# Gathered tokens of a product-key expert layer: joined to the output as rows, or turned and added in the closing stores

## The chip, the cores and the metric

The kernel runs on one core of a Trainium2 chip. The metric is the device time of one execution in microseconds (us), as the median of several runs. A profiled execution of the kernel before is read here as well; its own time stands beside its span below.

## What is computed

One decoder layer on 512 tokens of width 2048, all in float32. The part that matters here is its end: an expert feed-forward part (PEER) with 16384 experts, each one row of `expert_u` and one of `expert_v`, of which each token uses 8 x 16 = 128:

```python
x   = x + gate1 * (concat[y_c, y_a] @ W_out)              # called x1 in the kernel
h2  = RMSNorm(x) * (1 + scale2) + shift2
# idx, g: 128 experts and gates of each token, from product keys
a   = einsum('thkd,td->thk', expert_u[idx], h2)
ffn = einsum('thk,thkd->td', gelu(a) * g, expert_v[idx])
x   = x + gate2 * ffn
```

## The kernel before

Activations are kept transposed: a tile holds 128 of the 2048 features in its partitions and the tokens side by side. Every float32 product is made of three passes over a high and a low part (PASSES); `split` (L87) makes the two parts, the high one on ScalarE (L88), the low one by a subtraction on VectorE or GpSimd (L89).

**Stages.** Modulation and attention come first. Then the output projection (L529 to L561): four column groups dg of 512 features; each brings its part of x in, turns it (L535, L537, PSUM tiles `px` with two buffers), multiplies (L547), and forms x1 = x + gate1 * product on VectorE (L553), stored to `x1_dram` (L554) and squared for the norm (L559, L561). After the last group follow the sums of squares (L569), the root (L571, L572), its broadcast by eight small products into another `px` tile (L575), and h2 (L586 to L592). L586 overwrites x1 in place. Then come queries (L701) and selection of experts.

**Two ways for the expert part.** The 512 tokens are divided. The first TG = 160 are *gathered*: each fetches its own rows of the expert tables with indirect DMAs. The other TD = 352 are *dense*: all 16384 experts are multiplied with them, and a matrix W holds the gates.

The dense pass has 16 chunks of CH = 8 expert blocks. Of each block, `u_block` (L784) multiplies the turned rows of expert_u (loaded as `ur`, turned on VectorE L780, split) with h2 (L792), and `w_block` (L816) applies the gates and makes W. Then `v_group(ch, dg)` (L930) runs for the four column groups: four loads `vr` of expert_v (three buffers, L934), four splits `vs` (two buffers, L939), 24 products each (L945), summed in two PSUM tiles `pv` out of a pool of three (L924). The sums of the chunks are added up in `acc` (L959, L961).

Beside this, `steps` (L879) lists the gathers, and `gather_to` (L888) places them by the progress of the dense pass; each waits in GpSimd's queue for a product noted in `pace` (L847). A step fetches 128 half rows of 1024 values (512 KB) into one of four buffers `gt` (GBUF = 4, L843). The first group is tokens 0 to 127: 128 experts in two halves, first expert_u (dot products on VectorE, L853), then, after `gather_w`, expert_v (added up on VectorE into `gacc`, tokens in the partitions, L867 and L869). `gather_next` (L871) stores gacc to `a_dram` (L872) and loads what the second group needs. That group has the last nb = 32 gathered tokens, folded four times over the partitions: 32 experts for each quarter, so gacc then holds four partial sums of each token.

**The end.** In the last chunk, `begin(dg)` (L966) loads x1 of all tokens of a column group into `xs`, and adds acc times gate2 for the dense tokens (L972); after the group's products the last chunk's sums are added (L953). `add_gathered(dg)` (L975) reloads the first group's sums from a_dram (L978), turns them (L984), turns gacc (L988), copies both (L986, L989), adds the three other quarters (L991) and adds all to xs (L993). `store(dg)` (L996) turns xs back to rows (L1002, in a `pv` tile), copies (L1005 on VectorE, L1007 on ScalarE) and writes 512 columns of each 128 tokens out (L1008). ADD_AT and STORE_AT say after which dg this is done.

**What sets the order.** All loads and stores are issued by SP in one queue, the gathers by GpSimd. A planner (the tile framework) takes the program in the order in which it is written, estimates when each instruction can run, and fixes the order of every engine's queue; each engine then works through its queue in that order. Buffers of a pool are handed out in the order of the program. `add_manual_dep(..., ORDER)` tells the planner that one instruction comes after another.

## Time and profile before

| | |
|---|---|
| median of 3 runs | 3521.41 us (3520.7 to 3525.29) |
| the profiled execution | 3524.61 us, span 3522.6 us |
| mean granted TensorE clock | 0.967 |
| TensorE, VectorE, ScalarE, GpSimd busy | 92%, 81%, 35%, 40% |
| mean DMA rate over the span | 254 GB/s |
| output projection | about 795 to 967 us |
| first gather, first gather of the second group, last gather issued | 1455.0, 3072.3, 3458.0 us |

The span is the time from the first to the last instruction. Engines are PE (TensorE), DVE (VectorE), ACT (ScalarE), POOL (GpSimd) and SP, which only issues DMAs. A wait is put down to the instruction that released it last. [...]

### The profile page before, as it was taken

The page shows a single profiled execution, that of the slowest core. Times are in us where ns is not written, and L with a number is a line of the kernel's source. Part 1 is how long each engine was busy: PE and PEld are TensorE (multiplying, and loading weights), DVE is VectorE, ACT ScalarE, POOL GpSimd, SP SyncE. Part 2 cuts the span into 40 slices and gives each one's busy share as a digit, 9 for nine tenths or more (in the row PEclk, how much of TensorE's full clock was granted, in tenths as well). Part 3 has the DMA queues.
Part 4 walks back from the last instruction along what each step waited for, and adds up shares of the span by engine and source line. Part 5 has one row for each costly group of instructions (what it writes and reads, how often), then busy time and mean ns, then how long its engine had stood idle before and what let it go on. Part 6 is the DMA issues. An engine that isn't in the chain of part 4 may idle for free.

```text
span 3522.6 us, 49092 instructions
## 1 busy us (share of the span) xinstructions
PE 3223.4 (92%) x18006; PEld 2970.3 (84%) x18006; DVE 2847.1 (81%) x4261; ACT 1220.5 (35%) x1828; POOL 1417.5 (40%) x985
## 2 busy tenths in 40 slices
PE   5888999999998797999999999999999999999985
PEld 4766777677787686899998999889999999999975
DVE  6789766653269999789898888888999898988885
ACT  5232334343264357423232232223233232332221
POOL 2447332254447420134443444333434444444441
PEclk9999999999999899999999999999999999999987
DMA  8864755559722135899999999999999999999984
GB/s 288 286 229 143 254 190 178 183 177 290 252 88 68 61 122 202 264 298 323 305 315 295 310 310 299 300 287 300 306 314 313 298 307 306 326 310 319 299 302 163
DMA packets 425712, 896.34 MB, mean 254 GB/s; under 512 B 40402, under 2 KB 119167, under 8 KB 420735
## 3 DMA queue, kind: packets, MB, share of 16 engines
q1 hardware_dynamic: 333310, 557.62, 52.3%
q0 software_dynamic: 92160, 335.59, 29.3%
q8 instruction: 141, 2.31, 0.3%
q14 instruction: 101, 0.82, 0.1%
HBM read 843.47 MB, written 49.55 MB: 254 GB/s over the span
## 4 chain that ended last, share of the span: by engine, by line
DMA 42%; DVE 28%; PE 15%; issue 9%; POOL 3%; SPq 2%; ACT 1%; DVEq 0%; POOLq 0%; ACTq 0%
DMA ur<-in_expert_u_dram 14%; DMA vr<-in_expert_v_dram 9%; DMA gt<-in_expert_u_dram,idxu 6%; PE pm L457 4%; DMA ada_w<-in_w_ada_dram 4%; DMA gt<-in_expert_v_dram,idxu 4%; DVE gacc L869 3%; DVE utf L780 3%; DVE vs L89 2%; DVE gt L907 2%; DVE gt L853 2%; DVE ut L89 2%; DVE ada_acc L196 2%; PE pm L547 2%; DVE run L196 2%
## 5 line engine op out<-in xcount | busy, mean ns | idle before, releaser
L792 PE MATMUL pa<-hd,ut 128*128 128x352 f32 x6144 | 1077.3, 328 | 63.9 <-DVE ut L89 41.0
L945 PE MATMUL pv<-W,vs 128*128 128x352 f32 x6144 | 1071.4, 328 | 50.6 <-DVE vs L89 27.0
L792 PEld LDWEIGHTS pa<-hd,ut 128*128 128x128 f32 x6144 | 1015.2, 191 | 75.8 <-DVE ut L89 48.4
L945 PEld LDWEIGHTS pv<-W,vs 128*128 128x128 f32 x6144 | 1014.5, 191 | 61.2 <-DVE vs L89 32.7
L89 POOL TENSOR_TENSOR wsp<-wraw,wsp 128x1024 fp32r<-128x1024 f32 x160 | 391.5, 2449 | 562.1 <-ACT wsp L88 530.3
L844 POOL DMA_INDIRECT gt<-in_expert_u_dram,idxu x256 | 343.9, 1344 | 626.4 <-DVE gt L853 309.8
L88 ACT ACTIVATE vs<-vr 128x1024 fp32r<-128x1024 f32 x256 | 271.3, 1060 | 819.2 <-DMA vr<-in_expert_v_dram 365.8
L844 POOL DMA_INDIRECT gt<-in_expert_v_dram,idxu x256 | 340.0, 1328 | 477.9 <-DVE gacc L869 341.5
L853 DVE SCALAR_TENSOR_TENSOR gt<-gt,h2n 128x1024 f32<-128x1024 f32 x320 | 386.2, 1215 | 104.9 <-DMA gt<-in_expert_u_dram,idxu 84.8
L869 DVE SCALAR_TENSOR_TENSOR gacc<-gt,ga_a,gacc 128x1024 f32<-128x1024 f32 x316 | 400.4, 1275 | 73.9 <-DMA gt<-in_expert_v_dram,idxu 48.5
L89 DVE TENSOR_TENSOR vs<-vr,vs 128x1024 fp32r<-128x1024 f32 x256 | 309.8, 1210 | 46.9 <-ACT vs L88 46.7
L88 ACT ACTIVATE ut<-utf 128x1024 fp32r<-128x1024 f32 x232 | 244.0, 1056 | 282.3 <-DVE utf L780 169.6
L780 DVE STREAM_TRANSPOSE utf<-ur 128x1024 f32<-128x1024 f32 x232 | 286.9, 1237 | 18.2 <-DMA ur<-in_expert_u_dram 14.1
L88 ACT ACTIVATE wsp<-wraw 128x1024 fp32r<-128x1024 f32 x160 | 169.1, 1058 | 368.1 <-issue 94.7
L89 DVE TENSOR_TENSOR ut<-utf,ut 128x1024 fp32r<-128x1024 f32 x232 | 281.9, 1215 | 9.6 <-ACT ut L88 9.5
L457 PE MATMUL pm<-big,wsp 128*128 128x512 f32 x1152 | 287.6, 402 | 0.0
L457 PEld LDWEIGHTS pm<-big,wsp 128*128 128x128 f32 x1152 | 215.2, 192 | 42.6 <-issue 0.2
L196 DVE SCALAR_TENSOR_TENSOR ada_acc<-ada_w,scol,ada_acc 128x512 f32<-128x512 f32 x195 | 208.3, 1068 | 28.5 <-DMA ada_w<-in_w_ada_dram 25.1
L245 PE MATMUL pqk<-wsp,big 128*128 128x512 f32 x768 | 193.3, 411 | 21.3 <-DVE qk L291 12.9
L701 PE MATMUL pm<-big,wsp 128*128 128x512 f32 x768 | 188.2, 402 | 16.1 <-POOL wsp L89 14.5
L245 PEld LDWEIGHTS pqk<-wsp,big 128*128 128x128 f32 x768 | 150.6, 199 | 57.6 <-DVE qk L291 15.9
L701 PEld LDWEIGHTS pm<-big,wsp 128*128 128x128 f32 x768 | 146.2, 193 | 48.5 <-POOL wsp L89 17.0
(274 smaller groups left out, 3195.4 us busy)
## 6 DMA issues: line engine op xcount, KB each, us to landing
vr<-in_expert_v_dram SPq DMA_DIRECT2D x256, 512.0 KB, 10.0
ur<-in_expert_u_dram SPq DMA_DIRECT2D x928, 128.0 KB, 9.2
ada_w<-in_w_ada_dram SPq DMA_DIRECT2D x192, 512.0 KB, 4.6
wraw<-in_w_in_dram SPq DMA_DIRECT2D x96, 512.0 KB, 5.0
g_dram<-gtile SPq DMA_DIRECT2D x11, 2048.0 KB, 7.1
g<-g_dram SPq DMA_DIRECT2D x32, 704.0 KB, 13.6
wraw<-in_w_out_dram SPq DMA_DIRECT2D x32, 512.0 KB, 5.1
wraw<-in_w_peer_q_dram SPq DMA_DIRECT2D x32, 512.0 KB, 3.7
```

The costliest lines, as they stand in the source:

```text
L88: hi = nc.scalar.activation(dst[:, 0], src, AF.Copy)
L89: (eng or nc.vector).tensor_tensor(out=dst[:, 1], in0=src, in1=dst[:, 0].bitcast(F32), op=OP.subtract)
L196: nc.vector.scalar_tensor_tensor(new, wt[:, k], s, old, op0=OP.mult, op1=OP.add)
L245: nc.tensor.matmul(banks[i], hT[kk][:, a, i * P:(i + 1) * P], ws[:, b, k], start=(kk == last[0] and n == 0), stop=(kk == last[1] and n == 2))
L457: nc.tensor.matmul(banks[n2], ws[:, a, k, n2 * P:(n2 + 1) * P], hT[kk][:, b], start=(kk == 0 and n == 0), stop=(kk == KC - 1 and n == 2))
L701: nc.tensor.matmul(banks[j], ws[:, a, k, j * P:(j + 1) * P], h2T[kk][:, b], start=(kk == 0 and n == 0), stop=(kk == KC - 1 and n == 2))
L780: nc.vector.transpose(t, UR[0][:, :, q * 256:(q + 1) * 256].rearrange("p b (c r) -> p c b r", r=32))
L792: mm = nc.tensor.matmul(pa[:, :TD], ut[:, a, j], hd[k][:, b], start=(k == 0 and n == 0), stop=(k == KC - 1 and n == 2))
L844: d = nc.gpsimd.indirect_dma_start(out=t, out_offset=None, in_=src, in_offset=bass.IndirectOffsetOnAxis(ap=gidx[g][:, j:j + 1], axis=0), e ...
L853: nc.vector.scalar_tensor_tensor(t, t, 1.0, h2n[:, f * D // 2:(f + 1) * D // 2], op0=OP.mult, op1=OP.mult, accum_out=ga_a[:, f, j:j + 1])
L869: nc.vector.scalar_tensor_tensor(gacc[:, s], t, a, gacc[:, s], op0=OP.mult, op1=OP.add)
L945: mm = nc.tensor.matmul(pv[j // 2][:, j % 2, :TD], vs[:, a, bb, j * P:(j + 1) * P], W[e0 // 2][:, m, bb], start=(b == 0 and n == 0), stop= ...
```

## The change

Gathered tokens don't enter the closing stores any more. In the output projection a new `residual_rows(dg)`, called one group later, turns x1 of the 160 gathered tokens into rows and stores them (`x1n_dram`), and makes gate2 as rows, equal in all partitions, by products of a broadcast column with the identity (`g2_dram`). `gather_next` then finishes the first group's 128 tokens as rows on VectorE, with two `gt` buffers for each half, and writes them to the output, instead of storing gacc. The second group is finished in `settle`, after the last dense product: four products of gacc with `foldm` (four unit matrices of 32 one above the other) add the four quarters, and VectorE applies gate2 and x1. `begin`, `add_groups` and `store` handle the 352 dense tokens alone (three row tiles of 96, 128 and 128); xs is loaded one group earlier, and store(dg) comes one group later.

```diff
@@ -44,8 +44,6 @@
 WO_ORDER = (0, 1, 2, 3, 4, 5, 8, 9, 10, 11, 12, 13, 14, 15, 6, 7)
 UR_BUFS = 2
 BEGIN = 1
-ADD_AT = ((0,), (1,), (2,), (3,))
-STORE_AT = ((), (0,), (1,), (2, 3))
 RUN_MAX = 12
 TKJ = 2
 NPRE = 12
@@ -102,11 +100,14 @@
         g_dram = tc.dram_tile([TD // GB, NK, NK, GB], F32, name="g_dram")
         u_dram = tc.dram_tile([NPRE, P, D], F32, name="u_dram")
         h_dram = tc.dram_tile([TG - P, D], F32, name="h_dram")
-        a_dram = tc.dram_tile([P, D], F32, name="a_dram")
+        x1n_dram = tc.dram_tile([TG, D], F32, name="x1n_dram")
+        g2_dram = tc.dram_tile([P, D], F32, name="g2_dram")
 
         ident = const.tile([P, P], F32, name="ident")
         make_identity(nc, ident)
         modc = const.tile([P, 6, KC], F32, name="modc")
+        foldm = const.tile([P, TG - P], F32, name="foldm")
+        nc.vector.tensor_reduce(foldm, ident.rearrange("p (f t) -> p t f", t=TG - P), axis=AX.X, op=OP.add)
         big_ctx = ctx.enter_context(ExitStack())
         early = big_ctx.enter_context(tc.tile_pool(name="early", bufs=1))
         ones = early.tile([P, P], F32, name="ones")
@@ -524,6 +525,24 @@
                 u_quarter(t[:, q], ur, q)
             nc.sync.dma_start(u_dram[e], t.rearrange("p q c b r -> p (q c b r)"))
 
+
+        def residual_rows(dg):
+            for (t0, n) in ((0, P), (P, TG - P)):
+                t = px()
+                for j in range(4):
+                    nc.tensor.transpose(t[:n, j * P:(j + 1) * P], x1[dg * 4 + j][:, t0:t0 + n], ident)
+                r = xw.tile([P, T], F32, name="xn")
+                nc.scalar.activation(r[:n], t[:n], AF.Copy)
+                nc.sync.dma_start(x1n_dram[t0:t0 + n, dg * 512:(dg + 1) * 512], r[:n])
+            t = px()
+            for j in range(4):
+                k = dg * 4 + j
+                nc.tensor.matmul(t[:, j * P:(j + 1) * P], modc[:, 5, k:k + 1].to_broadcast([P, P]), ident,
+                                 start=True, stop=True)
+            r = xw.tile([P, T], F32, name="xn")
+            nc.scalar.activation(r, t, AF.Copy)
+            nc.sync.dma_start(g2_dram[:, dg * 512:(dg + 1) * 512], r)
+
         ahead = list(range(NPRE))
         sqs = x1p.tile([P, T], F32, name="sqs")
         for dg in range(4):
@@ -559,6 +578,9 @@
                     nc.scalar.activation(sq, xs, AF.Square)
                     if k < KC - 1:
                         nc.vector.tensor_tensor(out=sqs, in0=sqs, in1=sq, op=OP.add)
+            if dg:
+                residual_rows(dg - 1)
+        residual_rows(3)
 
         xy_ctx.close()
 
@@ -869,7 +891,15 @@
                 nc.vector.scalar_tensor_tensor(gacc[:, s], t, a, gacc[:, s], op0=OP.mult, op1=OP.add)
 
         def gather_next():
-            nc.sync.dma_start(a_dram, gacc)
+            for f in range(2):
+                s = slice(f * D // 2, (f + 1) * D // 2)
+                g2 = gp.tile([P, D // 2], F32, name="gt", bufs=GBUF)
+                nc.sync.dma_start(g2, g2_dram[:, s])
+                xn = gp.tile([P, D // 2], F32, name="gt", bufs=GBUF)
+                nc.sync.dma_start(xn, x1n_dram[0:P, s])
+                nc.vector.tensor_tensor(out=g2, in0=g2, in1=gacc[:, s], op=OP.mult)
+                nc.vector.tensor_tensor(out=g2, in0=g2, in1=xn, op=OP.add)
+                nc.sync.dma_start(out[0:P, s], g2)
             w = P // fold
             for f in range(fold):
                 nc.sync.dma_start(h2n[f * nb:(f + 1) * nb, :], h_dram)
@@ -934,8 +964,10 @@
                 vr = vp.tile([P, 2, 512], F32, name="vr", bufs=VR_BUFS)
                 ld = nc.sync.dma_start(vr, expert_v[e0 * P:(e0 + 2) * P, dg * 512:(dg + 1) * 512]
                                   .rearrange("(b p) d -> p b d", p=P))
-                if ch == nch - 1 and b2 == BEGIN:
-                    begin(dg, ld)
+                if ch == nch - 1 and dg == 0 and b2 == 0:
+                    begin(0, ld)
+                if ch == nch - 1 and dg < 3 and b2 == BEGIN:
+                    begin(dg + 1, ld)
                 vs = vp.tile([P, 2, 2, 512], F32R, name="vs", bufs=VS_BUFS)
                 split(vs, vr)
                 for j in range(4):
@@ -948,10 +980,12 @@
                 pace.append(mm)
                 gather_to(ch * CH + CH * 0.55 + (dg * (CH // 2) + b2 + 1) * 0.225)
             if ch == nch - 1:
+                if dg == 0:
+                    add_groups(0)
                 for j in range(4):
                     k = dg * 4 + j
-                    nc.vector.scalar_tensor_tensor(xs[dg][:, j, TG:], pv[j // 2][:, j % 2, :TD], modc[:, 5, k:k + 1],
-                                                   xs[dg][:, j, TG:], op0=OP.mult, op1=OP.add)
+                    nc.vector.scalar_tensor_tensor(xs[dg][:, j], pv[j // 2][:, j % 2, :TD], modc[:, 5, k:k + 1],
+                                                   xs[dg][:, j], op0=OP.mult, op1=OP.add)
             else:
                 for j in range(2):
                     k = dg * 4 + j * 2
@@ -964,48 +998,46 @@
         xs = [None] * 4
 
         def begin(dg, behind):
-            xs[dg] = fin.tile([P, 4, T], F32, name="xs", bufs=4)
-            t = nc.sync.dma_start(xs[dg], x1_dram[dg * 4:(dg + 1) * 4].rearrange("k p t -> p k t"))
+            xs[dg] = fin.tile([P, 4, TD], F32, name="xs", bufs=4)
+            t = nc.sync.dma_start(xs[dg], x1_dram[dg * 4:(dg + 1) * 4, :, TG:].rearrange("k p t -> p k t"))
             tc.add_manual_dep(t.ins, behind.ins.name, ORDER, reason="weights first")
+
+        def add_groups(dg):
             for j in range(4):
                 k = dg * 4 + j
-                nc.vector.scalar_tensor_tensor(xs[dg][:, j, TG:], acc[:, k], modc[:, 5, k:k + 1], xs[dg][:, j, TG:],
+                nc.vector.scalar_tensor_tensor(xs[dg][:, j], acc[:, k], modc[:, 5, k:k + 1], xs[dg][:, j],
                                                op0=OP.mult, op1=OP.add)
 
-        def add_gathered(dg):
-            if NG == 2:
-                ar = fin.tile([P, 512], F32, name="ar")
-                nc.sync.dma_start(ar, a_dram[:, dg * 512:(dg + 1) * 512])
-            else:
-                ar = gacc[:, dg * 512:(dg + 1) * 512]
-            for j in range(4):
-                k = dg * 4 + j
-                pt = psA.tile([P, T], F32, name="pa").rearrange("p (j t) -> p j t", t=P)
-                nc.tensor.transpose(pt[:, 0], ar[:, j * P:(j + 1) * P], ident)
-                ft = fin.tile([P, TG], F32, name="ft")
-                nc.scalar.activation(ft[:, 0:P], pt[:, 0], AF.Copy)
-                if NG == 2:
-                    nc.tensor.transpose(pt[:, 1], gacc[:, k * P:(k + 1) * P], ident)
-                    nc.scalar.activation(ft[:, P:], pt[:, 1, 0:nb], AF.Copy)
-                    for f in range(1, fold):
-                        nc.vector.tensor_tensor(out=ft[:, P:], in0=ft[:, P:],
-                                                in1=pt[:, 1, f * nb:(f + 1) * nb], op=OP.add)
-                nc.vector.scalar_tensor_tensor(xs[dg][:, j, 0:TG], ft, modc[:, 5, k:k + 1], xs[dg][:, j, 0:TG],
-                                               op0=OP.mult, op1=OP.add)
-
         def store(dg):
-            for i in range(NT):
-                if i % 2 == 0:
+            t0 = TG
+            for i in range(TG // P, NT):
+                n = (i + 1) * P - t0
+                if (i - TG // P) % 2 == 0:
                     pq = psV.tile([P, 2, T], F32, name="pv")
-                po = pq[:, i % 2]
+                po = pq[:n, (i - TG // P) % 2]
                 for j in range(4):
-                    nc.tensor.transpose(po[:, j * P:(j + 1) * P], xs[dg][:, j, i * P:(i + 1) * P], ident)
+                    nc.tensor.transpose(po[:, j * P:(j + 1) * P], xs[dg][:, j, t0 - TG:t0 - TG + n], ident)
                 ot = fin.tile([P, T], F32, name="ot", bufs=4)
                 if i % 2:
-                    nc.vector.tensor_copy(ot, po)
+                    nc.vector.tensor_copy(ot[:n], po)
                 else:
-                    nc.scalar.activation(ot, po, AF.Copy)
-                nc.sync.dma_start(out[i * P:(i + 1) * P, dg * 512:(dg + 1) * 512], ot)
+                    nc.scalar.activation(ot[:n], po, AF.Copy)
+                nc.sync.dma_start(out[t0:t0 + n, dg * 512:(dg + 1) * 512], ot[:n])
+                t0 += n
+
+
+        def settle():
+            g2 = fin.tile([nb, D], F32, name="g2", bufs=1)
+            nc.sync.dma_start(g2, g2_dram[0:nb])
+            nc.sync.dma_start(h2n[0:nb], x1n_dram[P:TG])
+            for c in range(4):
+                s = slice(c * 512, (c + 1) * 512)
+                ps = psA.tile([P, T], F32, name="pa")
+                mm = nc.tensor.matmul(ps[:nb], foldm, gacc[:, s], start=True, stop=True)
+                tc.add_manual_dep(mm.ins, pace[-1].ins.name, ORDER, reason="products of the dense tokens first")
+                nc.vector.tensor_tensor(out=g2[:, s], in0=ps[:nb], in1=g2[:, s], op=OP.mult)
+                nc.vector.tensor_tensor(out=g2[:, s], in0=g2[:, s], in1=h2n[0:nb, s], op=OP.add)
+                nc.sync.dma_start(out[P:TG, s], g2[:, s])
 
         nch = NK // CH
         fin = None
@@ -1022,10 +1054,12 @@
             for dg in range(4):
                 v_group(ch, dg)
                 if ch == nch - 1:
-                    for f in ADD_AT[dg]:
-                        add_gathered(f)
-                    for f in STORE_AT[dg]:
-                        store(f)
+                    if dg < 3:
+                        add_groups(dg + 1)
+                    if dg:
+                        store(dg - 1)
+        settle()
+        store(3)
 
 
 # ---- launch: one core; inputs and outputs as the reference has them ----
```

## Rows read from the trace of the kernel before

**Rows 1.** The page's busy times, first row: busy us (share of the span) and number of products.

```profile
...
PE 3223.4 (92%) x18006; PEld 2970.3 (84%) x18006; DVE 2847.1 (81%) x4261; ACT 1220.5 (35%) x1828; POOL 1417.5 (40%) x985
...
```

**Rows 2.** Busy time of each engine in stretches of the dense pass and of the end: the stretch, its length, then busy us and number of instructions of PE, of its weight loads, of DVE, ACT and POOL; the granted TensorE clock; the DMA engines' busy share; GB/s.

```profile
...
3000.00:3100.00 100.00, 99.95 (x622) 99.67 (x621) 92.93 (x89) 29.90 (x34) 48.43 (x33) 1.00 1.05 332
3300.00:3400.00 100.00, 92.93 (x565) 91.92 (x564) 91.65 (x82) 27.27 (x31) 47.71 (x37) 0.98 0.94 299
...
3430.00:3465.00 35.00, 1.22 (x6) 0.53 (x4) 24.30 (x27) 1.45 (x3) 17.54 (x12) 0.55 0.72 252
3465.00:3523.00 58.00, 47.63 (x284) 44.50 (x284) 29.26 (x89) 15.32 (x42) 0.00 (x0) 0.88 0.36 127
...
```

**Rows 3.** Who waited for whom from 3390 us to the end: us in total, times, longest.

```profile
...
PE pa L988 <- DVE gacc L869: 32.4, 1, 32.4
...
DVE gacc L869 <- DMA gt<-in_expert_v_dram,ib: 17.7, 13, 4.3
...
```

**Rows 4.** VectorE's instructions in order of time, 3425 to 3482 us: start, us, the instruction, how many in a row, and what its idle time before was ended by. The row that starts at 3444.37 is followed by nine more accumulations before that at 3463.59.

```profile
...
3427.82 1.23 DVE L89 TENSOR_TENSOR vs<-vr,vs 128x1024 fp32r<-128x1024 f32 x1 [2.54 <-ACT vs L88]
...
3432.13 1.21 DVE L89 TENSOR_TENSOR vs<-vr,vs 128x1024 fp32r<-128x1024 f32 x1
...
3435.24 4.86 DVE L869 SCALAR_TENSOR_TENSOR gacc<-gt,ga_a,gacc 128x1024 f32<-128x1024 f32 x4
3444.37 1.28 DVE L869 SCALAR_TENSOR_TENSOR gacc<-gt,ga_a,gacc 128x1024 f32<-128x1024 f32 x1 [4.27 <-DMA gt<-in_expert_v_dram,ib]
...
3463.59 1.29 DVE L869 SCALAR_TENSOR_TENSOR gacc<-gt,ga_a,gacc 128x1024 f32<-128x1024 f32 x1 [0.70 <-DMA gt<-in_expert_v_dram,ib]
...
3478.99 1.22 DVE L89 TENSOR_TENSOR vs<-vr,vs 128x1024 fp32r<-128x1024 f32 x1 [2.09 <-ACT vs L88]
...
```

**Rows 5.** TensorE's products in order of time, 3425 to 3470 us, same columns.

```profile
...
3424.59 5.94 PE L945 MATMUL pv<-W,vs 128*128 128x352 f32 x31
3462.95 0.69 PE L988 MATMUL pa<-ident,gacc 128*128 128x128 f32 x2 [32.41 <-DVE gacc L869]
...
```

**Rows 6.** Groups of instructions by line from 3430 us to the end: how many, busy us, mean ns of one, idle us before.

```profile
...
L945 PE MATMUL pv<-W,vs 128*128 128x352 f32 x196 | 36.5, 344 | 0.0
...
L1002 PE MATMUL pv<-ident,xs 128*128 128x128 f32 x64 | 11.8, 310 | 3.8 <-DVE xs L953 1.5 <-DVE xs L993 1.3 <-ACT ot L1007 0.9
...
L991 DVE TENSOR_TENSOR ft<-ft,pa 128x32 f32<-128x32 f32 x48 | 6.4, 184 | 7.5 <-ACT ft L989 7.2
...
L988 PE MATMUL pa<-ident,gacc 128*128 128x128 f32 x16 | 3.9, 304 | 33.4 <-DVE gacc L869 32.4 <-ACT ft L986 1.0
...
```

**Rows 7.** VectorE's instructions in order of time from 3505 us to the end, columns as in rows 4.

```profile
...
3510.54 1.07 DVE L953 SCALAR_TENSOR_TENSOR xs<-pv,modc,xs 128x352 f32<-128x352 f32 x2 [0.53 <-PE pv L945]
...
3518.06 1.29 DVE L1005 COPY ot<-pv 128x512 f32<-128x512 f32 x2 [1.87 <-ACT ot L1007]
```

**Rows 8.** All engines in order of time around the change of groups, 3050 to 3125 us, columns as in rows 4; SPq is the queue that issues loads and stores.

```profile
...
3070.70 1.29 DVE L869 SCALAR_TENSOR_TENSOR gacc<-gt,ga_a,gacc 128x1024 f32<-128x1024 f32 x1 [1.16 <-DMA gt<-in_expert_v_dram,idxu]
...
3072.26 0.94 POOL L844 DMA_INDIRECT gt<-in_expert_u_dram,ib  x1 [1.90 <-DVE gacc L869]
...
3078.09 2.48 DVE L869 SCALAR_TENSOR_TENSOR gacc<-gt,ga_a,gacc 128x1024 f32<-128x1024 f32 x2
...
3086.07 0.35 SPq L872 DMA_DIRECT2D a_dram<-gacc  x1
...
```

**Rows 9.** The page's DMA issues: how many, KB each, median us from issue to landing.

```profile
...
vr<-in_expert_v_dram SPq DMA_DIRECT2D x256, 512.0 KB, 10.0
...
x_dram<-x SPq DMA_DIRECT2D x16, 256.0 KB, 4.3
...
out_dram<-ot SPq DMA_DIRECT2D x16, 256.0 KB, 2.3
...
a_dram<-gacc SPq DMA_DIRECT2D x1, 1024.0 KB, 12.0
...
```

**Rows 10.** The gathers' instructions on GpSimd (L844) in two stretches of the dense pass: the stretch, its length, busy us (number), granted clock, DMA share, GB/s.

```profile
...
2400.00:2800.00 400.00, 166.37 (x127) 0.99 1.04 307
2800.00:3200.00 400.00, 172.67 (x127) 0.99 1.03 311
...
```

**Rows 11.** Groups of instructions by line in the output projection, 795 to 973 us, columns as in rows 6.

```profile
...
L547 PE MATMUL pm<-big,wsp 128*128 128x512 f32 x691 | 161.2, 393 | 5.9 <-DVE x L553 5.9
...
L553 DVE SCALAR_TENSOR_TENSOR x<-pm,modc,x 128x512 f32<-128x512 f32 x16 | 11.4, 739 | 30.7 <-PE pm L547 30.6
...
L537 ACT ACTIVATE x<-px 128x512 f32<-128x512 f32 x16 | 9.0, 589 | 5.0 <-PE px L535 5.0
...
```

**Rows 12.** TensorE's products in order of time around the end of the output projection, columns as in rows 5.

```profile
...
968.58 0.38 PE L569 MATMUL sp<-ones,sqs 128*128 128x1 f32 x2 [1.44 <-DVE sqs L561]
...
971.24 1.19 PE L575 MATMUL px<-ident,rc 128*128 128x128 f32 x8 [0.66 <-DVE rc L572]
...
```

**Rows 13.** What GpSimd waited for from 1900 to 3060 us: us in total, times, longest.

```profile
...
POOL gt L844 <- DVE gacc L869: 338.8, 164, 9.4
...
POOL gt L844 <- PE pv L945: 30.9, 17, 4.1
...
```

**Rows 14.** The gathers of the whole span (line L844): landing times.

```profile
...
DMA to landing us min/median/max: 4.2/9.2/13.2
```

## The prediction

> **What bounds the kernel now.** I read the page's busy shares first, then the windows of the dense pass and of the end, then the waits of the last 130 us, then the order of the instructions around the longest of these waits. TensorE is busy for 92% of the span [rows 1], and in the dense pass this is real work: 622 products in 100 us, one each 0.161 us, with the DMA queues as full [rows 2]. No other stage than the end shows a hole. There, from 3430 to 3465 us, TensorE does 1.2 us of work in 35, and its granted clock has fallen to 0.55; then come 58 us with the DMA share at 0.36 [rows 2]. The waits name the cause: one wait of 32.4 us of the transposes of gacc (L988) for VectorE's last accumulation (L869) [rows 3]. The order shows why it costs so much. On VectorE two splits of the third column group's weights start at 3427.8 and 3432.1, then fifteen accumulations follow, the last at 3463.6, and the next split only at 3479.0 [rows 4]; on TensorE the L988 pair stands right behind the last product of the second column group [rows 5]. So half of the last chunk's dense products (two of four column groups, 2 x 4 x 24 = 192; the view has 196 records with neighbours [rows 6]) stand behind the gathers. The kernel's end is therefore gathers, then 192 products, then stores, one after the other: 3465 plus 58.
>
> **The sum is made against** the profiled execution: span 3522.6 us, run 3524.61, which is 2.0 more; the median of the runs is 3521.41, 3.2 below that run. I take both differences over.
>
> **Removed at the end.** All that lies between the gathered sums and the dense columns: 16 L988 transposes, as many of the reloaded first group, 48 small adds (6.4 us of VectorE), and 20 of 64 store transposes (11.8 us for 64) [rows 6]. Most of it lies between products, so I book it at nothing of its own. What counts is that no dense instruction depends on gacc any more: store(0), whose PSUM bank the third column group takes over, now holds dense tokens only, and settle's products are told to follow the last dense one. TensorE should go on at 3430 with its 192 products: 192 x 0.161 = 31 us, then 12 us from the last product (3510.5) to the end of the span as now [rows 7], so the dense side alone would end near 3430 + 31 + 12 = 3473. What is late next is the gathers themselves.
>
> **Added in the output projection.** Per column group 8 transposes, 4 products with the identity, three copies on ScalarE and three DMA writes. Eight such 128-wide products take 1.19 us [rows 12], so 48 take 7 us at most; TensorE loses 5.9 us at the group seams anyway [rows 11], which the rows of the first two groups can fill. The last group's rows fall into the one serial place: sums of squares at 968.6, the broadcast at 971.2 [rows 12], with the same two PSUM buffers. There 8 transposes and two copies of 0.59 us [rows 11] come first: 1.2 + 1.2, I take 3 us. Ends: 0 if the planner fits all into seams; 16 if it doesn't: 7 us of TensorE and two turns of the pair of row buffers, each held by a store of 4.3 us [rows 9]. Taken: **+3**, since the nearest rows (12) show idle gaps there of the size needed. Nothing later gives this back, because the selection that follows is a chain of its own. The constant for the fold is one small VectorE instruction at the very start, covered by the first weight loads: nothing.
>
> **Added amid the dense pass.** gather_next now issues, on SP, four loads and two stores of 512 KB where one store of 1 MB stood, and four VectorE instructions of the shape of an accumulation, 1.28 us each [rows 4]: 5 us, and 2 MB more, 7 us at 300 GB/s. While it runs the gathers pause and leave their share free, so I take **+2** (0 to 7). The wait it adds matters more. The four tiles are the gathers' own four buffers. Today the second group's first gather starts at 3072.3, when the buffer before the last two is free, before the last two accumulations of the first group (3078.1 to 3080.6) are done [rows 8]. Afterwards that buffer takes the gate row (issued 3072), its neighbour the residual (3076); a 512 KB load lands after 10.0 us [rows 9], so product and sum are done at 3088, the store has landed by 3097 (1 MB took 12.0 [rows 9]), and only then is the buffer free: a **hole of 25 us** in the gather stream. Queued behind these waits are, on SP, the loads of ur and vr that TensorE needs next; a_dram today slips in between such loads within 6 us of the last accumulation [rows 8], and the buffers ahead of TensorE (two ur, three vr) cover that much. If this cover is gone, each microsecond of SP's wait is one of TensorE's. Does the stream catch up? It moves one gather per 3.1 us (127 in 400 us [rows 10]), and its waits before the second group are 339 us for a buffer held by VectorE against 31 for the pace of the V products [rows 13]: it is not held back by its pace, so the hole stays. Eight gathers (25 / 3.1) move to the end.
>
> The fastest landing of a gather is 4.2 us [rows 14]; with that in each step the hole is 14 us. [...]
>
> **The end, then.** From 3430 to 3465 the queues moved 35 us x 252 GB/s = 8.8 MB [rows 2]. Before the last gather lands there come in addition: the eight gathers (4.2 MB), three loads of vr (1.6), the last xs (0.7), settle's two loads (0.5), and the stores of three column groups (2.2): 18.0 MB in all. At 300 GB/s, which the pass shows [rows 2], that is 60 us: the last accumulation ends near **3490** (3501 at 252 GB/s). Then settle: four products, eight VectorE operations on 512 columns at 0.74 us [rows 11], two of the four strips overlapping the last accumulation, and a store that lands after 2.3 us [rows 9]: 8 us, **3498**. With +3 and +2: span 3503, run 3505, median **3502**.
>
> **Rivals.**
> *The hole closes or is cheap.* Without it 8.8 + 5.0 = 13.8 MB, 46 us, 3476; settle 3484; +5; median 3488. For it: VectorE has the room of the eight gathers to run ahead in. Against: rows 10 and 13. Chance 0.20.
> *VectorE's order keeps the products behind (slower).* Taking the transposes off TensorE frees nothing if VectorE, in the planner's order, still has the last accumulations ahead of the splits. Two splits went ahead and six came after [rows 4]. With six behind, the dense side ends at 3490 + 6 x 24 x 0.161 + 12 = 3525, +5, median 3529: the hole is then paid in full. It decides from six; with five or fewer it is no loss that can be measured. [...] What speaks against six: a split waits for its buffer to be free of products, and these now run on at 4 us per split, against 2.0 us per accumulation (fifteen from 3435 to 3465 [rows 4]), so the planner finds splits ready amid the accumulations. Chance 0.15.
> *The gain is spent ahead of the end.* The output projection pays 16 instead of 3: 3515, no difference that a measurement shows. Chance 0.13.
> That the change doesn't do what it says, TensorE waiting for gathers again, I exclude for all but settle, whose products stand last by an explicit order.
>
> **How the numbers follow.** About 0.2% (7 us) is what a measurement of this kernel can tell from no change: faster is below 3514, slower above 3528. The forecast has 0.52; nearly all of it (0.48) is faster, the rest same. The cheap hole adds 0.20, faster. The third rival is same. So faster 0.68, same 0.17, slower 0.15. The range runs from 3482 (cheap hole, and nothing lost in the projection: 3485, with 3 us for the seams filled) to 3528, just short of the slower rival.
>
> **What would show it.** Right: no long wait of TensorE between 3430 and the end; VectorE's splits of the last two groups between accumulations; the last accumulation 20 to 30 us later than 3465; a break in POOL's gathers of some 25 us around 3080, longer than any neighbour; the selection stage shifted by some 3 us. Wrong: splits behind the last accumulation, gathers ending by 3475, a TensorE hole near 3090, or a projection later by over 10 us.

## The result, and the profile after

The changed kernel is slower: **3554.2 us** (median of 6 runs, 3546.68 to 3561.16) against 3521.3 us (6 runs, 3503.56 to 3525.29), a ratio of 1.0102 [1.0078, 1.0126]. The forecast was 3502 us. The profiled execution took 3551.79 us, its span is 3549.2 us, 26.6 longer than before.

The stretches of [rows 2] in the changed kernel, columns as there (the granted clock is a share of the full one):

```profile
...
3000.00:3100.00 100.00, 95.78 (x574) 94.91 (x573) 90.81 (x82) 29.83 (x35) 41.47 (x32) 0.97 1.03 310
3300.00:3400.00 100.00, 90.78 (x544) 88.30 (x543) 82.59 (x92) 28.72 (x33) 38.06 (x30) 0.98 1.03 291
3430.00:3465.00 35.00, 23.77 (x128) 22.60 (x126) 25.50 (x24) 5.84 (x7) 17.05 (x14) 0.84 0.84 290
3465.00:3549.00 84.00, 61.08 (x330) 53.68 (x330) 68.29 (x83) 13.02 (x14) 33.91 (x22) 0.86 0.74 251
...
```

The idle stretch from 3430 to 3465 is filled (23.8 us of TensorE's work, not 1.2), and the end runs with a DMA share of 0.74 where it had 0.36. The waits from 3390 us to the end, as in [rows 3]:

```profile
...
DVE gacc L891 <- DMA gt<-in_expert_v_dram,ib: 24.4, 16, 4.2
...
PE pv L977 <- DVE vs L87: 9.3, 5, 5.7
...
```

The 32.4 us wait of [rows 3] is gone; what is late now is the gathers' landing. VectorE's order, answering to [rows 4, 7] (start, us, instruction, number in a row, idle time before):

```profile
...
3451.01 1.22 DVE L87 TENSOR_TENSOR vs<-vr,vs 128x1024 fp32r<-128x1024 f32 x1
3452.14 1.28 DVE L891 SCALAR_TENSOR_TENSOR gacc<-gt,ga_a,gacc 128x1024 f32<-128x1024 f32 x1
...
3466.25 1.22 DVE L87 TENSOR_TENSOR vs<-vr,vs 128x1024 fp32r<-128x1024 f32 x1
...
3521.19 1.22 DVE L87 TENSOR_TENSOR vs<-vr,vs 128x1024 fp32r<-128x1024 f32 x1
...
3539.78 1.28 DVE L891 SCALAR_TENSOR_TENSOR gacc<-gt,ga_a,gacc 128x1024 f32<-128x1024 f32 x1
...
3545.28 1.27 DVE L1039 TENSOR_TENSOR g<-g,h2n 32x512 f32<-32x512 f32 x2
...
```

Splits and accumulations take turns up to the last split at 3521, and settle ends 8 us after the last accumulation at 3541. So the end works as intended, but that accumulation, at 3463.6 before [rows 4], starts 76 us later. The change of groups, answering to [rows 8] (all engines):

```profile
...
3106.40 1.68 POOL L866 DMA_INDIRECT gt<-in_expert_v_dram,idxu  x1 [0.65 <-DVE gacc L891]
...
3113.25 0.34 SPq L897 DMA_DIRECT2D gt<-g_dram  x1
...
3115.61 2.47 DVE L891 SCALAR_TENSOR_TENSOR gacc<-gt,ga_a,gacc 128x1024 f32<-128x1024 f32 x2
...
3120.65 0.35 SPq L899 DMA_DIRECT2D gt<-x1n_dram  x1
...
3122.94 1.23 DVE L900 TENSOR_TENSOR gt<-gt,gacc 128x1024 f32<-128x1024 f32 x1 [2.56 <-DMA gt<-g_dram]
...
3128.29 1.21 DVE L901 TENSOR_TENSOR gt<-gt 128x1024 f32<-128x1024 f32 x1
3129.77 0.94 POOL L866 DMA_INDIRECT gt<-in_expert_u_dram,ib  x1 [21.69 <-DVE gt L901]
...
3130.99 0.36 SPq L902 DMA_DIRECT2D out_dram<-gt  x1
...
3140.88 0.94 POOL L866 DMA_INDIRECT gt<-in_expert_u_dram,ib  x1 [10.17 <-DMA ur<-in_expert_u_dram]
...
```

There is the hole: one wait of 21.7 us, ended by the sum with the residual (L901). The gather after it starts 11 us later: its buffer is the gate row's, whose store (L902) was issued at 3131.0. (The view puts this wait down to a load of `ur`, but releasers are inferred.) And the end of the output projection, answering to [rows 12] (all engines):

```profile
...
976.78 0.38 PE L591 MATMUL sp<-ones,sqs 128*128 128x1 f32 x2 [0.57 <-DVE sqs L580]
...
980.39 0.60 ACT L543 ACTIVATE xn<-px 128x512 f32<-128x512 f32 x1 [2.44 <-DMA x1n_dram<-xn]
...
984.70 2.07 PE L597 MATMUL px<-ident,rc 128*128 128x128 f32 x8 [0.92 <-ACT xn L535]
...
```

The broadcast starts at 984.7, not 971.2. **A ledger** of the shift of common milestones (start of the same instruction after, minus before):

| up to | shift, us | step, us |
|---|---|---|
| first V product (1446.5 before) | +9.4 | +9.4 |
| gather number 500 (3037.3) | +36.4 | **+27.0** |
| gather 516, behind the hole (3085.1) | +61.9 | +25.5 |
| last gather issued (3458.0) | +76.3 | +14.4 |
| end of the span (3522.6) | +26.6 | -49.7 |

The second row is the surprise: 1600 us of dense pass in which the change has no instruction, and in which every engine's instructions stand in the same order as before. The one difference found there is where the tiles lie. `foldm` holds 128 bytes in each partition and is allocated ahead of everything on the left side of the on-chip memory: gacc, gt, W, ur, utf, ut, g4 and ge, all at multiples of 512 bytes before, lie 128 bytes further on.

### The profile page after: what moved, and what is told of

Read it like the earlier page. It is cut to its first block, busy times and chain, and to the rows that moved or that the text cites. A ratio compares the mean times of both kernels' runs of the same rounds, so it can differ in the third digit from the quotient of the medians.

```text
span 3549.2 us, 49080 instructions
## 1 busy us (share of the span) xinstructions
PE 3250.5 (92%) x18030; PEld 2984.8 (84%) x18030; DVE 2844.7 (80%) x4210; ACT 1217.6 (34%) x1803; POOL 1414.4 (40%) x985
## 4 chain that ended last, share of the span: by engine, by line
DMA 40%; DVE 27%; PE 18%; issue 10%; POOL 3%; SPq 1%; ACT 1%; DVEq 0%; POOLq 0%; ACTq 0%
DMA ur<-in_expert_u_dram 10%; DMA vr<-in_expert_v_dram 8%; PE pm L458 5%; DMA ada_w<-in_w_ada_dram 4%; DMA gt<-in_expert_u_dram,idxu 4%; DMA gt<-in_expert_v_dram,idxu 3%; PE pa L814 3%; DMA g<-g_dram 3%; DVE ada_acc L197 2%; DVE gacc L891 2%; POOL gt L866 2%; DVE vs L87 2%; DVE utf L802 2%; DMA gt<-in_expert_u_dram,ib 2%; DVE ut L87 2%
## 5 line engine op out<-in xcount | busy, mean ns | idle before, releaser
L866 POOL DMA_INDIRECT gt<-in_expert_u_dram,idxu x256 | 336.4, 1314 | 654.7 <-DVE gt L875 314.3
L86 ACT ACTIVATE ut<-utf 128x1024 fp32r<-128x1024 f32 x232 | 244.3, 1055 | 279.7 <-DVE utf L802 151.1
L458 PE MATMUL pm<-big,wsp 128*128 128x512 f32 x1152 | 288.8, 403 | 0.0
L458 PEld LDWEIGHTS pm<-big,wsp 128*128 128x128 f32 x1152 | 216.3, 193 | 43.0 <-issue 0.2
L723 PE MATMUL pm<-big,wsp 128*128 128x512 f32 x768 | 187.4, 402 | 11.4 <-POOL wsp L87 9.8
L566 PE MATMUL pm<-big,wsp 128*128 128x512 f32 x768 | 183.5, 398 | 7.8 <-DVE x L572 7.8
```

The costliest lines, as they stand in the source:

```text
L86: hi = nc.scalar.activation(dst[:, 0], src, AF.Copy)
L458: nc.tensor.matmul(banks[n2], ws[:, a, k, n2 * P:(n2 + 1) * P], hT[kk][:, b], start=(kk == 0 and n == 0), stop=(kk == KC - 1 and n == 2))
L723: nc.tensor.matmul(banks[j], ws[:, a, k, j * P:(j + 1) * P], h2T[kk][:, b], start=(kk == 0 and n == 0), stop=(kk == KC - 1 and n == 2))
L866: d = nc.gpsimd.indirect_dma_start(out=t, out_offset=None, in_=src, in_offset=bass.IndirectOffsetOnAxis(ap=gidx[g][:, j:j + 1], axis=0), e ...
```

## The experiments

Medians in us; the ratio is to the kernel before, run beside them on the same chip (3523.8 us for experiments 1 to 4, 3525.69 for 5 to 8, 3526.49 for 9 to 12). A ratio is taken over all runs, so it can differ a little from that of the medians.

**1. The rows alone.** The kernel before, with residual_rows called as in the change; nothing uses them.

```diff
...
+            if dg:
+                residual_rows(dg - 1)
+        residual_rows(3)
```

> The kernel before, plus the making of the rows in the output projection (their values are read by nobody). In the trace of the changed kernel the dense pass began 9.4 us later than before, and then lost another 27 us up to the 500th gather although every engine's instructions stood in the same order. Theory 1 (the loss comes with the rows: their two new tensors in DRAM, or the later start): 9 + 27, near 3557 us. Theory 2 (it comes with the new constant that moves all other tiles in SBUF, absent here): 9 alone, near 3530.

Measured: 3538.99 (12 runs), 1.0039 [1.0012, 1.0065]: **+14 us** (4 to 23), where the expectation had 9. TensorE's products of the output projection, from 795 to 978 us, columns as in [rows 11]; then its end, all engines in order of time:

```profile
...
L566 PE MATMUL pm<-big,wsp 128*128 128x512 f32 x683 | 163.2, 399 | 9.5 <-DVE x L572 9.5
...
```

```profile
...
977.16 0.38 PE L591 MATMUL sp<-ones,sqs 128*128 128x1 f32 x2 [0.57 <-DVE sqs L580]
...
980.54 0.60 ACT L543 ACTIVATE xn<-px 128x512 f32<-128x512 f32 x1 [2.21 <-DMA x1n_dram<-xn]
...
984.37 0.59 ACT L535 ACTIVATE xn<-px 32x512 f32<-32x512 f32 x1 [2.60 <-DMA g_dram<-xn]
...
985.01 1.16 PE L597 MATMUL px<-ident,rc 128*128 128x128 f32 x8 [1.17 <-ACT xn L535]
...
```

The sums of squares already start 8.6 us later than in [rows 12]: up to the last product of the projection TensorE is busy for 4.9 us longer, and its waits at the group seams didn't shrink but grew, from the 5.9 us of [rows 11] to 9.5. Another 5.2 us lie between the sums of squares and the broadcast (7.8 us apart, 2.7 before): there two turns of the pair of row buffers stand, each held by a store. Together that delays L586, the first instruction behind the broadcast, by 13.7 us, the first V product by 15.5; from there to gather 500 this kernel loses nothing (-3). The rows cost nearly what the upper bound in the prediction said, and they are not the dense pass's loss.

**2. The fold constant alone.** The kernel before, with `foldm` made and not used.

```diff
+        foldm = const.tile([P, TG - P], F32, name="foldm")
+        nc.vector.tensor_reduce(foldm, ident.rearrange("p (f t) -> p t f", t=TG - P), axis=AX.X, op=OP.add)
```

> The kernel before, plus the constant for the fold (32 columns in SBUF ahead of every other tile, and one small VectorE instruction), used by nobody. Theory 2 (moved tiles): the dense pass loses 27 us, near 3548. Theory 1 (rows): no difference, 3521. A third theory, that the loss is a state of a particular build or run and belongs to no part: anything between, and the dense passes of e1 and e2 don't fit either theory.

Measured: 3578.02 (6 runs), **1.0153** [1.011, 1.0196]: +54 us for one small instruction and 128 bytes, twice what was expected. The expectation counted up to gather 500; in the profile the first V product comes at the same time (-0.3) and gather 500 29 us later, but another 16 us are lost from there to the last gather. Three of the page's costliest groups (line, tiles, count, busy, mean ns, idle before and its releaser), first of the kernel before, then of this one:

```profile
...
L88 ACT ACTIVATE vs<-vr 128x1024 fp32r<-128x1024 f32 x256 | 271.3, 1060 | 819.2 <-DMA vr<-in_expert_v_dram 365.8
...
L780 DVE STREAM_TRANSPOSE utf<-ur 128x1024 f32<-128x1024 f32 x232 | 286.9, 1237 | 18.2 <-DMA ur<-in_expert_u_dram 14.1
...
L89 DVE TENSOR_TENSOR ut<-utf,ut 128x1024 fp32r<-128x1024 f32 x232 | 281.9, 1215 | 9.6 <-ACT ut L88 9.5
...
```

```profile
...
L88 ACT ACTIVATE vs<-vr 128x1024 fp32r<-128x1024 f32 x256 | 271.2, 1060 | 888.3 <-DMA vr<-in_expert_v_dram 511.7
...
L782 DVE STREAM_TRANSPOSE utf<-ur 128x1024 f32<-128x1024 f32 x232 | 287.1, 1238 | 36.8 <-DMA ur<-in_expert_u_dram 28.3
...
L89 DVE TENSOR_TENSOR ut<-utf,ut 128x1024 fp32r<-128x1024 f32 x232 | 282.2, 1216 | 10.5 <-ACT ut L88 10.4
...
```

VectorE works on the shifted tiles as fast as before (1238 and 1216 ns against 1237 and 1215), ScalarE too (1055 ns on `ut` against 1056, from 1600 to 3000 us; the vs and vr of the first line lie on the right side and did not move). What grows is the idle time that ends with a DMA (for `vr` from 365.8 to 511.7 us, for `ur` from 14.1 to 28.3). TensorE reads shifted tiles too, and is no slower for it: in the same stretch a product takes 328 ns (expert_u) and 327 ns (expert_v) against 327 and 326, a weight load 190 and 190 against 191 and 190. So it is the loads that came later, and not the instructions that were slower.

**3. Without the hole.** The changed kernel; gacc goes to a_dram as before, and the first group is finished in the last chunk in tiles of its own, in halves.

```diff
         def gather_next():
-            for f in range(2):
...
+            nc.sync.dma_start(a_dram, gacc)
...
+                    if 0 < dg < 3:
+                        first_group(dg - 1)
```

> The changed kernel, but the first group is not finished between the groups: gacc is stored as in the kernel before, and both halves are finished as rows in the last chunk from tiles of their own. Theory A (the hole of about 24 us in the gather stream comes from the finishing in the gathers' own buffers, and the end waits for the gathers): the hole falls under 8 us, the last accumulation comes some 20 us earlier, total 3525 to 3535. Rival B (the end is set by the dense products, the hole is hidden): less than 7 us gained, 3547 or more.

Measured: 3562.52 (10 runs), 1.0097 [1.0068, 1.0125]: the gap between gathers 511 and 512 fell to 4.1 us, and the time did not fall with it (theory A had 3525 to 3535).

**4. Without the rows.** The changed kernel with rows of the input read in their place (it leaves out the residual rows, so residual and gate are other numbers).

```diff
...
-            if dg:
-                residual_rows(dg - 1)
-        residual_rows(3)
...
-                nc.sync.dma_start(xn, x1n_dram[0:P, s])
+                nc.sync.dma_start(xn, x[0:P, s])
```

> The changed kernel without the making of the rows; the finishing reads rows of the input x of the same sizes in their place (so residual and gate are other numbers), and the two tensors in DRAM are gone. The start of the dense pass should be back to before, 9 us gained in every theory. Theory 1 (the dense loss comes with the rows): a further 27, near 3518. Theory 2 (it comes with the constant, which stays): near 3545.

Measured: 3563.02 (7 runs), 1.0094 [1.0058, 1.013]. The first V product comes only 1.8 us later than before, and that brings nothing that shows (theory 2 had 3545). The profiles of experiments 3 and 4 lose 54 to 55 us from the first V product to gather 500 where the changed kernel's lost 27. Experiments 3 and 4 are inconclusive as they stand: as long as the tiles are shifted, a cost of that size, and not the same in every kernel, lies on top of what is to be measured.

**5. The fold constant and 384 bytes.** Experiment 2 with a pad that brings the shift to 512 bytes.

```diff
+        pad = const.tile([P, 96], F32, name="pad")
+        nc.vector.memset(pad, 0.0)
```

> The kernel before with the constant for the fold, as e2, and 384 bytes more of an unused constant behind it, so that all tiles of the gathers and of the loads of expert_u lie 512 bytes later than before, and not 128. Theory 2a (what costs is the alignment: the destinations of gathers and ur begin at multiples of 512 bytes before, and 128 behind one in e2): back at before, 3515 to 3532. Theory 2b (any moved address or any added instruction at the start costs): near e2, 3570 or more.

Measured: 3526.15 (11 runs), 0.9995 [0.9975, 1.0015]. One instruction and 384 bytes more, and the whole loss is gone. It was the address.

**6. The V side moved to multiples of 512.** On the right side, h2n, hd, acc, vr and vs stood 224 bytes behind a multiple of 256 all along; a pad of 224 bytes moves them in the kernel before (vr, vs and acc onto multiples of 512, h2n and hd onto multiples of 256).

```diff
         h2n = ga.tile([P, D], F32, name="h2n")
+        padr = ga.tile([P, 56], F32, name="padr")
+        nc.vector.memset(padr, 0.0)
```

> The kernel before, with 224 bytes of an unused tile at the other end of SBUF, which moves vr, vs, acc and hd from 224 bytes behind a multiple of 512 onto one. Theory 2a (alignment of the destination of a load): the loads of expert_v land earlier, and the dense pass, where queues and TensorE are both full, gains 10 to 40 us: 3485 to 3515. Rival (only gathers and ur are sensitive, or the pass is bound by TensorE): no difference, 3515 to 3530.

Measured: 3510.17 (8 runs), **0.9953** [0.9931, 0.9974]: the kernel before had a loss of the same kind in it. The stretch from 1600 to 3000 us of the dense pass (length, busy and number of PE, its weight loads, DVE, ACT, POOL; clock; DMA share; GB/s), first in the kernel before, then with the constant (2), then with the V side moved (6):

```profile
...
1600.00:3000.00 1400.00, 1338.98 (x8126) 1325.53 (x8125) 1245.41 (x1340) 416.23 (x467) 596.01 (x445) 0.98 1.03 305
...
```

```profile
...
1600.00:3000.00 1400.00, 1326.61 (x8011) 1309.51 (x8009) 1225.28 (x1321) 406.20 (x457) 582.28 (x438) 0.98 1.03 300
...
```

```profile
...
1600.00:3000.00 1400.00, 1354.96 (x8284) 1344.56 (x8283) 1268.99 (x1364) 424.59 (x476) 614.12 (x455) 0.99 1.02 311
...
```

The DMA engines are as busy in all three (1.02 to 1.03), and move 305, 300 and 311 GB/s; TensorE does 8126, 8011 and 8284 products in the same 1400 us. So the same transfers, into other addresses, took more of the DMA engines' time here. TensorE's own rate hardly moves here either (326 and 325 ns a product).

**7. The whole change, padded.** The pad of experiment 5 in the changed kernel.

> The changed kernel with 384 bytes of an unused constant behind the one for the fold, so that the gathers' and ur's destinations begin at multiples of 512 bytes again. Theory 2a: the 27 us that the dense pass lost before the change of groups come back, and what remains is 9 from the rows and the hole, against what the end gains: 3515 to 3530. Theory 2b: 3545 or more.

Measured: **3510.21** (11 runs), **0.9955** [0.993, 0.9979]. The change as meant is faster than before by 16 us, a little more than expected, and the 128 bytes cost it 44 us by the medians (3554.2 - 3510.2), 52 by the ratios. GpSimd's order of time at the change of groups, then VectorE's at the end:

```profile
...
3082.69 1.68 POOL L868 DMA_INDIRECT gt<-in_expert_v_dram,idxu  x1 [0.65 <-DVE gacc L893]
3107.44 0.94 POOL L868 DMA_INDIRECT gt<-in_expert_u_dram,ib  x1 [23.07 <-DVE gt L903]
...
```

```profile
...
3505.67 1.28 DVE L893 SCALAR_TENSOR_TENSOR gacc<-gt,ga_a,gacc 128x1024 f32<-128x1024 f32 x1 [0.39 <-DMA gt<-in_expert_v_dram,ib]
...
3510.70 1.27 DVE L1041 TENSOR_TENSOR g<-g,h2n 32x512 f32<-32x512 f32 x2
...
```

Its ledger beside that of the changed kernel: +18.2 at the first V product, then -4.7, +25.6 for the hole, +3.0, and -50.1 in the tail. The padding takes away both losses of the dense pass (27.0 and 14.4) and leaves hole and tail as they were.

**8. All together.** The changed kernel with both pads, without the hole, and with the rows' buffers kept apart from the broadcast's (four row buffers, the `sp` tiles of PSUM, the last group's rows behind the broadcast).

> The changed kernel with the alignment of e5 and e6, without the hole (first group finished in the last chunk from tiles of its own, in quarters), and with the rows made through other PSUM tiles and four row buffers, those of the last column group behind the broadcast of the norm. If alignment, hole and serial place are the three losses: 3554 less 27, less 24, less 9, less what e6 gains, near 3490 (3470 to 3505). If the hole was covered by the dense products, as e3 suggests: 3505 to 3520.

Measured: **3491.68** (5 runs), 0.9888 [0.986, 0.9916], the fastest kernel here. The broadcast still came 11.0 us late and the first V product 11.4. TensorE's order there:

```profile
...
978.08 0.38 PE L593 MATMUL sp<-ones,sqs 128*128 128x1 f32 x2
...
980.51 1.95 PE L536 MATMUL sp<-ident,x 128*128 128x128 f32 x8
982.25 1.91 PE L599 MATMUL px<-ident,rc 128*128 128x128 f32 x8
...
```

The sums of squares came 9.5 us late, as in experiment 1, and the broadcast 4.2 us behind them, not 7.8. So the buffers kept apart gave back most of the 5.2 us at the serial place, though the planner still put the last group's turns (L536) ahead of the broadcast; the larger part of the rows' cost lies before, in the projection itself, and nothing here took it away.

**9. Without the hole, padded.** Experiment 3 with the pad, and with the first group finished in quarters, not halves.

> The changed kernel with 384 bytes of padding behind the fold constant (all tiles of the left side again at multiples of 512 bytes), and with the first group finished in the last chunk from a copy of its sums, not between the two groups' gathers. With the pad alone the changed kernel took 3510 us. Theory A (the hole of about 21 us between gathers 511 and 512 delays the last accumulation one for one): the gap falls to 4 us, the last accumulation comes about 17 to 20 us earlier, the time is 3490 to 3496 us. Rival B (as without the pad, where taking the hole away gave nothing that could be measured: the gathers catch up or the dense work in the last chunk grows by as much): 3505 to 3515 us, the accumulations end where they ended with the hole.

Measured: 3495.99 (5 runs), 0.99 [0.9869, 0.993]: 14 us less than experiment 7 by the medians, 19 by the ratios (the intervals touch at 0.993). That speaks for theory A. GpSimd at the change of groups, then VectorE's last accumulation:

```profile
...
3071.75 1.68 POOL L869 DMA_INDIRECT gt<-in_expert_v_dram,idxu  x1 [0.66 <-DVE gacc L894]
3076.69 0.94 POOL L869 DMA_INDIRECT gt<-in_expert_u_dram,ib  x1 [3.26 <-DVE gacc L894]
...
```

```profile
...
3484.22 1.27 DVE L894 SCALAR_TENSOR_TENSOR gacc<-gt,ga_a,gacc 128x1024 f32<-128x1024 f32 x1
...
```

The last accumulation starts at 3484, 21 us before that of experiment 7. The last gather's shift says what is given back: from +3.6 behind the change of groups to +20.1 at the end, since the first group's loads and stores now stand in the last chunk. So taking the hole away does gain once the tiles are aligned; what hid the gain in experiment 3, whose dense pass lost twice what the changed kernel's did, stays open.

**10 to 12. Which destinations, and which step.** The kernel before with a pad of 128 bytes in front of one pool alone, or with everything on the left shifted by 256.

```diff
         up = up_ctx.enter_context(tc.tile_pool(name="up", bufs=2))
+        padu = up.tile([P, 32], F32, name="padu", bufs=1)
...
         gp = ctx.enter_context(tc.tile_pool(name="gp", bufs=1))
+        padg = gp.tile([P, 32], F32, name="padg")
...
+        padh = gp.tile([P, 96], F32, name="padh")
...
+        foldm = const.tile([P, TG - P], F32, name="foldm")
+        pad = const.tile([P, 32], F32, name="pad")
```

> The kernel before with 128 bytes in front of the U weights' pool alone: ur, utf, ut, g4 and ge stand at 128 behind a multiple of 512 bytes; the gathers' tiles, gacc and W stay at multiples of 512. Theory L (the loads of the U weights, the larger stream, pay for it): landing of ur rises by about 0.6 us (from 9.7 us), the time by 25 to 50 us over before (3550 to 3575 us). Rival G (the gathers' destinations pay): ur lands as before, the time is within 8 us of before (3518 to 3534 us).

> The kernel before with 128 bytes in front of gacc and the gathers' tiles alone, and 96 floats behind them, so that W and the U weights stay at multiples of 512 bytes. Theory L (the U weights' loads pay): within 8 us of before (3518 to 3534 us). Rival G (the gathers' destinations, four tiles of 4 KB per partition in turn, pay): the gathers land 0.5 us or more later, and the time rises by 25 to 50 us (3550 to 3575 us). If both halves pay, this one and the other rise by parts that add up to the 52 us of the whole shift.

> The kernel before with the fold constant and 128 bytes of padding, so that every tile of the left side stands at 256 behind a multiple of 512 bytes (128 behind cost 52 us, 512 behind nothing). Theory of 256 (what counts is whether a destination begins at a multiple of 256 bytes): within 8 us of before, 3518 to 3534 us. Rival of 512 (only multiples of 512 are cheap): 3560 to 3590 us, as at 128. [...]

Measured: the U weights' pool by 128: 3565.27 (5 runs), 1.0096 [1.0068, 1.0124], +34 by the ratio. The gathers' pool by 128: 3550.6 (11 runs), 1.0068 [1.0045, 1.0091], +24. Everything by 256: 3526.02 (11 runs), 1.0004 [0.9971, 1.0037], nothing. Both streams pay, +58 together against the +54 of the whole shift. Of the shifts of the whole left side that were run, 128 bytes cost 54 us (experiment 2), and 256 and 512 (experiment 5) nothing that shows: here it was enough that the destinations began at multiples of 256 bytes. The stretch from 1600 to 3000 us again, in the same order:

```profile
...
1600.00:3000.00 1400.00, 1326.29 (x8020) 1311.70 (x8019) 1228.31 (x1327) 408.83 (x459) 591.00 (x440) 0.98 1.02 301
...
```

```profile
...
1600.00:3000.00 1400.00, 1333.53 (x8068) 1321.12 (x8069) 1237.16 (x1337) 415.48 (x467) 592.68 (x442) 0.98 1.02 303
...
```

```profile
...
1600.00:3000.00 1400.00, 1337.84 (x8122) 1326.18 (x8122) 1244.32 (x1342) 416.27 (x468) 598.04 (x445) 0.98 1.02 305
...
```

301, 303 and 305 GB/s at one busy share: the order of the times, though the kernel of experiment 1, with the same addresses as before, shows 307. Neither this nor the landing times, by which the expectations would have told the streams apart, does so: ur's median landing in this stretch was 9.5 us before and 9.8, 10.0 and 9.8 in these three. The queues' own rates do. In the same stretch, q0 with the gathers and q1 with the plain loads and stores (packets, MB, share of the 16 engines' time), first before, then with the U weights' pool shifted, then with the gathers' pool shifted:

```profile
...
q0 software_dynamic: 63873, 232.59, 52.1%
q1 hardware_dynamic: 129897, 192.90, 50.0%
...
```

```profile
...
q0 software_dynamic: 63249, 230.33, 51.5%
q1 hardware_dynamic: 128170, 189.86, 50.4%
...
```

```profile
...
q0 software_dynamic: 63750, 232.13, 52.7%
q1 hardware_dynamic: 128775, 190.92, 49.1%
...
```

For the time that its packets take (192.90 MB in 50.0% of 1400 us), q1 moves 276 GB/s before, 269 with the U weights shifted and 278 with the gathers shifted; q0 moves 319, 319 and 315. Each queue is slower where its own destinations are shifted, and the other isn't. For q1 that is well outside what the kernels with the left side in place show (276 to 279), for q0 just outside (316 to 322). The gathers, and not the loads of the U weights as the expectation has it, are the larger stream. The V side shows in the same way, q1 in experiments 6 and 8:

```profile
...
q1 hardware_dynamic: 132973, 196.49, 49.6%
...
```

```profile
...
q1 hardware_dynamic: 130149, 193.53, 48.9%
...
```

That is 283 GB/s in both.

Why 128 bytes cost time and 256 don't is not shown by these runs.

## Why the prediction was wrong

- **The step that failed** is the last sentence on the output projection: "The constant for the fold is one small VectorE instruction at the very start, covered by the first weight loads: nothing." The instruction does cost nothing (experiment 5). Its tile costs 44 us or more in the changed kernel and 54 in the one before (experiments 7 and 2), because it moves every tile behind it to 128 bytes behind a multiple of 256, where loads and gathers moved fewer GB/s: q1 269 against 276 with the U weights' pool shifted, q0 315 against 319 with the gathers' (experiments 10 and 11). The sum priced instructions, transfers and waits, and had no term for where the tiles lie.
- **The rows** were mis-sized: +3 taken from the idle gaps of [rows 12], +14 measured alone (experiment 1), close to the upper end of 16. What failed here is that the rows of the first groups would fill TensorE's 5.9 us at the seams: the waits there grew to 9.5, and 8.6 us were lost before the sums of squares. Only 5.2 came from the two row buffers, each held by a store of [rows 9]'s kind, at the serial place of the broadcast. The bound of 7 us for TensorE was itself too low: the eight records of [rows 12] are four products, each of which shows as two (the 16 gate products of the changed kernel show as 32 records, L540), so by experiment 1's 1.03 us for a group's turns and 1.15 for its gate products it is 8.7 us for four groups.
- With 14 for the rows in place of 3 the sum is 3513, against 3510.2 for the change without the shift (experiment 7): the third rival, "spent ahead of the end", at 3515, is in size what the change as meant comes to. With experiment 2's 54 on top it would be 3567, 13 more than measured; the shift's cost isn't the same in every kernel.
- **The hole** was right in size, 25 us forecast and 25.5 in the ledger, and the gathers did not catch up; but in part that was luck. The first buffer to come free is the residual's, by the sum at 3129.5, and not the gate row's after its store, which holds the second gather instead. Against that, the rows' loads were issued 7 and 14 us after the last gather of the first group (3106.4), where the forecast has 3 and 7. The gate row's load landed in 9.7 us (issued 3113.25, its product waits until 3122.94), near the 10.0 of [rows 9]. The hole's worth to the time, 3502 - 3488 = 14 us between forecast and first rival, was 14 to 19 (experiments 7 and 9).
- **The tail** was right: the wait of [rows 3] went, the dense products filled it, the gathers' last accumulation sets the end, settle takes 8 us. The splits did not stay behind the gathers; the slower rival's mechanism did not occur, and the slower result came from elsewhere. In the padded kernel the last accumulation came at 3507 against 3495 forecast (3490 plus the sum's 5), 12 later: the rows' 11 and 1.
- **+2 for the dense pass** at the change of groups can't be told from zero: TensorE is idle for 2.7 of 60 us there (3100 to 3160), for 0.7 before (3065 to 3125), but for 5.3 in experiment 9 (3068 to 3128), which doesn't finish the rows there.
- **What bounds the dense pass** was read as TensorE's work, with the queues as full beside it, and no term follows from the second half. [rows 2] show TensorE 93 to 99.95% busy; yet a loss of 1.6% in the queues' rate (305 to 300 GB/s) came through in full: over the 1591 us from the first V product to gather 500 that is an estimated 26 us, and experiment 2 lost 29.
- That 20 of the 64 store transposes go is a count by tokens: 16 go, and 16 get narrower. It was booked at nothing, and nothing rests on it.

Open: why the shift costs 27 us up to gather 500 in one profile of the changed kernel and 54 to 55 in those of experiments 3 and 4 (302 GB/s from 1600 to 3000 us against 297 and 295); which of the tiles moved in experiment 6 brings its 16 us; and why the V side's move, worth 16 us in the kernel before, leaves only 4 between experiments 9 and 8, with q1 as fast in 8 as in 6; and what in the projection the rows' first 8.6 us could be hidden behind.

## What to carry to other kernels

Before pricing a new tile at nothing, look at what is allocated behind it and where the destinations of the large streams come to lie: here 128 bytes behind a multiple of 256 cost 54 us (experiment 2), and the pad that brought them back to multiples of 512 cost nothing (0.9995, experiment 5). The trace showed the loss as fewer GB/s at the same DMA busy share (300 against 305 at 1.03) and as longer waits for loads (511.7 us against 365.8 for `vr`), in no instruction. When a change with no instruction in a stage slows that stage and the order of the instructions is unchanged, compare the addresses. And don't book new side work at the idle gaps that it might fill: here the gaps grew (from 5.9 to 9.5 us), and only a run with the side work alone told its price. Where it shares buffers with a serial chain, count the stores that hold them as well (two turns of the row buffers, 5.2 us here).

## What the runs showed of the hardware

With the destinations of the U weights' loads and of the gathers 128 bytes behind a multiple of 256 in each partition, the kernel before took longer (3578.0 against 3523.8 us); with them at a multiple of 256 that is not one of 512 it did not (3526.0 against 3526.5). At the same DMA busy share of 1.02 to 1.03, from 1600 to 3000 us, the profiles with all of the left side shifted by 128 move 295 to 302 GB/s, those with it at multiples of 256 and the V side as it was 305 to 309; with the V side at multiples of 256 as well, it is 311 and 308. Instructions on the shifted tiles took the same time (experiment 2): VectorE 1216 against 1215 ns, ScalarE 1055 against 1056 (L88 on `ut`, 1600 to 3000 us), TensorE 328 against 327 ns a product.
